# A hybrid attention and MoE block: when the softmax denominators are inverted, and how many at once

## The chip, the cores and the metric

The kernel runs on one core of one Trainium2 chip. The metric is device time in microseconds (us) of one execution, as the median of several runs. The core has a matrix engine (TensorE, PE), three elementwise engines (VectorE or DVE, ScalarE or ACT, GpSimd or POOL) and SyncE (SP), which issues DMA transfers. Each engine runs its own instructions in the order in which the program wrote them, and waits for others by semaphores.

## What is computed

One transformer block over 1024 tokens of width 1024. Two attention branches work on the same modulated input, are projected, gated, summed and projected once more; a mixture of experts follows. What matters here are the two softmaxes:

```python
# branch A: 4 heads, each with two maps m = 0, 1, over all visible keys
logits = jnp.where(visible, logits + bias[None, :, None], -jnp.inf)
p = jax.nn.softmax(logits, axis=-1)
attn = p[:, :, 0] - lam * p[:, :, 1]
return jnp.einsum('bhqs,bshe->bqhe', attn.astype(v.dtype), v)
# branch B: 8 heads, over the 256 keys that an indexer picked for the query
logits = jnp.where(sel_ok[:, None], logits - slopes[...] * dist[:, None], -jnp.inf)
p = jax.nn.softmax(logits, axis=-1)
return jnp.einsum('bhqk,bqkr->bqhr', p.astype(kv_sel.dtype), kv_sel)
# then
mixed = g[:, :, 0] * (y_a @ w_a_proj[l]) + g[:, :, 1] * (y_b @ w_b_proj[l])
x = _layer_norm(DEEPNORM_ALPHA * x + gate1 * (mixed @ w_o[l]), ln1_g[l], ln1_b[l])
```

A softmax needs the sum of each row's exponentials inverted. Branch A needs the inverse of two sums per row before it can subtract the maps. Branch B multiplies after the values: its output is scaled by the inverse sums.

## The kernel before

Everything is fp32. A product of two fp32 matrices is made as three matmuls (lines 142, 145, 146) of operands split into a high and a low part; `copy` makes the high part, mostly on ACT, and `sub` (line 128) the low part on DVE. A row block is 128 queries, so there are 8 of them, and a row of scores with a block's number `qb` has (qb + 1) x 128 columns.

**Branch A** (336 to 641 us of the span). `a_attend` (line 870) works head by head. For each of the 8 blocks `softmax_pair` makes the scores of both maps (PE `plg`), adds the bias and takes the row's extreme on DVE (line 762), and takes the exponential on ACT with the row's sum as a by-product (line 765). Then, per row block: a reciprocal of the first sum (line 879), a copy of the first map scaled by it on ACT (880), a reciprocal of the second sum (881), its product with minus lambda (`nlam`, 882), both of one column, and the subtraction of the maps over the whole row on DVE (883). PE turns the result by `ptr` (line 793), ACT and DVE split it (`pth`, `ptl`), and PE multiplies with the values (`py`). This work is woven (`weave`, with weights for each step) with the projections (`pj`) that branch B and the gates need; a scheduler sets the order of each engine's instructions from the order in which they are written and its own estimate of their durations.

At the end of the weave stand the last head of branch A, the last projections, and preparations of later stages, which the scheduler has pulled ahead: `gb`, a table of 128 x 8 modulation values, which is loaded from `mod_d` in DRAM (line 1355) and gets 1 added on DVE (line 1356); `wl`, the low half of projection weights; `hl`, the split of a projection for branch B's queries, written to DRAM as `bq` (lines 256, 257); `br` and `mod_d`, rows of the modulation (lines 710, 711).

**Branch B** (`b_stage`, line 939, 641 to 829 us). Eight heads in four pairs. Here the order is planned by hand: each step is a `node` with an engine, a duration, a priority and the nodes that it depends on, and takes and gives back buffers; the planner takes the node that can start earliest by these numbers, and of equals the one of the smallest priority. The instructions are then issued in just that order. Per row block: the scores (`plg`, lines 994 to 997), bias and extreme on DVE (1001), exponential on ACT with the sum (1014), a reciprocal of one column on DVE into `rden`, a table of 128 x 8 blocks x 8 heads (1017). Per two row blocks: `ptr` (1037), the split, and the values `pyb` (1054, 1055), then the output `yb` (1074). When a pair of heads is done, `scale(c)` (line 1084) spreads the inverse sums of half the rows over 128 x 512 elements (`rr`, line 1094), PE turns that (`pbc`, 1099), DVE multiplies the output with it (1103), and it is split into `ybh` and `ybl`. `of_pair` lists the nodes that `scale` depends on.

The planner also has **fill**, nodes of the lowest priority that PE is to do while it waits: the norm of branch A's output (`ya`, loaded from DRAM at line 1130, its PE step at 1146, its DVE step at 1150; `yah` and `yal` are its halves), and the first half of the output projection of branch A (`pab`, line 1198, 192 matmuls of 128 x 512), with `gate` at 1207.

**After branch B** comes the other half of that projection (`pab<-ybh`, lines 142 to 146), with weights `wab` that are loaded to a buffer of tag `wr` (two buffers), issued on ACT's queue (line 217). The two `rr` tiles use the same two buffers, so that load waits for the last `pbc`.

Of the kernel before, what the change touches and what calls it, by code (L numbers as in the profile page):

```python
# [19 lines left out]
AF = mybir.ActivationFunctionType  # L20
OP = mybir.AluOpType
# [65 lines left out]
def block_kernel(ctx: ExitStack, tc, a, out):  # L87
    nc = tc.nc
    V, S, G, PE = nc.vector, nc.scalar, nc.gpsimd, nc.tensor
# [8 lines left out]
    def s4(name, tag, shape=(128, 1024), dt=FT):  # L98
        return sb.tile(list(shape), dt, name=name, tag=tag, bufs=SLOTS[tag])
# [19 lines left out]
    def tiny(name, w=8, dt=FT, bufs=8, tag=None):  # L119
        return sb.tile([128, w], dt, name=name, tag=f"tiny{w}{tag or ''}", bufs=bufs)  # L120
# [618 lines left out]
    nlam = cp.tile([128, 1], FT, name="nlam")  # L739
# [9 lines left out]

    def softmax_pair(q, k, qs, bias, L):  # L750

        Ps, mx = [s4("P", "P") for _ in range(2)], [tiny("mx") for _ in range(2)]
        for n_, (c0, n) in enumerate(pieces(L)):
            ps_ = [bank("plg", "lg") for _ in range(2)]
            for m, (a_, b_) in enumerate(((1, 0), (0, 1), (0, 0))):
                for s, p in enumerate(ps_):
                    r = slice(64 * s, 64 * s + 64)
                    i = PE.matmul(p[:, :n], q[a_][r, qs], k[b_][r, c0:c0 + n], start=m == 0, stop=m == 2)  # L758
                    if m == 0:
                        leads(i)  # L760
            for P, mx_, p in zip(Ps, mx, ps_):
                V.tensor_tensor_reduce(P[:, c0:c0 + n], p[:, :n], bias[:, c0:c0 + n], 1.0, mx_[:, 5:6] if n_ else 3.0e38,  # L762
                                       OP.add, OP.min, mx_[:, 0:1] if n_ or L <= 512 else mx_[:, 5:6])
        for P, mx_ in zip(Ps, mx):
            S.activation(P[:, :L], P[:, :L], AF.Exp, bias=mx_[:, 0:1], scale=-1.0, accum_out=mx_[:, 1:2])  # L765
        return list(zip(Ps, mx))

    def softmax_rows(q, hh, ll, bias, L, sel=None):

# [100 lines left out]
    def a_attend(h):  # L870
        q, k, vh, vl = A.pop(h)
        bias = bias_tile(SL_A[h])

        def rows(qb):
            L = (qb + 1) * 128
            bv = bias[:, 896 - 128 * qb:1024]
            qs = slice(qb * 128, qb * 128 + 128)
            (P0, m0), (P1, m1) = softmax_pair(q, k, qs, bv, L)
            V.reciprocal(m0[:, 2:3], m0[:, 1:2])
            S.activation(P0[:, :L], P0[:, :L], AF.Copy, scale=m0[:, 2:3])  # L880
            V.reciprocal(m1[:, 2:3], m1[:, 1:2])
            V.tensor_tensor(m1[:, 3:4], m1[:, 2:3], nlam, op=OP.mult)
            V.scalar_tensor_tensor(P0[:, :L], P1[:, :L], m1[:, 3:4], P0[:, :L], op0=OP.mult, op1=OP.add)
            return P0

        def tail(i, Ps):
            y = bank("py", "av", (128, 256))
            last = 2 * i + 1
            for kb, c0, n, th, tl in transposed_pairs(Ps, i):
                if kb % 2 == 0 and kb:  # L890
                    yield True
                if kb == min(2, last):
                    mean_squares()
                kv_ = slice(kb * 128, kb * 128 + 128)
                mm3(y[:, c0:c0 + n], vh[:, kv_], vl[:, kv_], th, tl, kb == 0, kb == last)
            yo = sb.tile([128, 256], FT, name="yo", tag="yo", bufs=2)
            copy(yo, y)
            dma(ya_d[h, :, i * 256:i * 256 + 256], yo)
            sq = sb.tile([128, 256], FT, name="yq", tag="yo", bufs=2)
            V.tensor_scalar(sq, yo, 1.84e19, -1.84e19, op0=OP.min, op1=OP.max)  # L900
            S.activation(sq, sq, AF.Square)
            squares.append((h, i, sq))
            yield True

        return pipelined(rows, tail)


# [31 lines left out]
    def b_stage():  # L939
# [15 lines left out]
        def head(n):  # L955
            nonlocal prev_bias
            c, s = heads[n]
# [18 lines left out]
            def row(qb):  # L976
# [34 lines left out]

                def exp():
                    P, mx = st["P"], st["mx"]
                    S.activation(P[:, :L], P[:, :L], AF.Exp, bias=mx[:, 0:1], scale=-1.0, accum_out=mx[:, 1:2])  # L1014

                e = node("ACT", 0.42 + 0.00095 * L, prio, mins, exp)
                of_pair.append(node("DVE", 0.1, prio + 4, [e], lambda: V.reciprocal(rden[:, qb, n:n + 1], st["mx"][:, 1:2])))
                return st, e

            def tail(i, rows_):  # L1020
# [63 lines left out]
        def scale(c, prio, y):  # L1084
            for half in range(2):
# [3 lines left out]
                def spread(half=half, z=z):  # L1089
                    if half == 0:  # L1090
                        ybh[c], ybl[c] = s4("ybh", "L", dt=FR), s4("ybl", "L", dt=FR)
                    z["rr"] = s2("rr", "wr")
                    rr = rden[:, half * 4:half * 4 + 4, 2 * c:2 * c + 2].unsqueeze(3).to_broadcast([128, 4, 2, 64])
                    copy(z["rr"].rearrange("p (j s e) -> p j s e", j=4, s=2), rr, V)

                def turn(z=z):
# [1 line left out]
                    for j in range(4):  # L1098
                        PE.transpose(z["p"][:, j * 128:j * 128 + 128], z["rr"][:, j * 128:j * 128 + 128], ident)

                f = node("DVE", 0.45, prio, y, spread, take=("wr",))
                b = node("PE", 0.46, prio, [f], turn, take=("tp",), give=(("wr", f),))
                d = node("DVE", 0.69, prio, [b], lambda t=t, z=z: V.tensor_tensor(ybs[c][:, t], ybs[c][:, t], z["p"], op=OP.mult),
                         give=(("tp", b),))
# [967 lines left out]
```

## Time and profile before

| | us |
|---|---|
| median of 3 runs | 1365.82 |
| the 3 runs | 1362.2, 1365.85, 1365.82 |
| the profiled execution | 1362.08 |
| its span | 1360.3 |

| engine | busy us | share of the span |
|---|---|---|
| PE | 1228.1 | 90% |
| DVE | 950.2 | 70% |
| ACT | 665.4 | 49% |
| POOL | 128.1 | 9% |

The busy shares are averages over stages of different kinds. From 30 to 607 us PE is hardly ever idle. It idles around branch B's start and end, and again in the experts, from 850 us on. PE's clock was granted at full speed for 95.6% of the time. The profiled execution is one of the shorter ones, 3.7 us under the median.

### The profile page before, as it was taken

Reading aid. Unit: us, or ns where it says so; the run is one execution under the profiler, and the core shown is the slowest. Engines: PE = TensorE matmul, PEld = TensorE weight load, DVE = VectorE, ACT = ScalarE, POOL = GpSimd, SP = SyncE. Lnnn points to the kernel's source line nnn. Section 1 sums busy time; section 2 is a strip of 40 time slices with the busy share of each in tenths; the row PEclk is TensorE's granted clock in tenths of the full one; section 3 lists DMA queues with packets and bytes.
Section 4 is the critical chain, followed back from the end, with each engine's and each line's share of the span. In section 5 each row is a group of like instructions: output and inputs, shape, how many; then the busy total and the mean of one; then the engine's idle time right before and its main releaser. Section 6 shows DMA issues by size and latency. Waiting matters only on the chain.

```text
span 1360.3 us, 18426 instructions
## 1 busy us (share of the span) xinstructions
PE 1228.1 (90%) x6184; PEld 969.7 (71%) x6199; DVE 950.2 (70%) x2065; ACT 665.4 (49%) x1189; POOL 128.1 (9%) x154
## 2 busy tenths in 40 slices
PE   8999999999999999999699997898985898999940
PEld 6876678877777778677578886677873677788830
DVE  6537789783456757672698886677786778777736
ACT  4536662213785555453677762324224565555405
POOL 1000000000000001010011000000002233232210
PEclk9999999999999999999899998898996999999975
DMA  9202452123124326683455525564436789989756
GB/s 364 101 32 70 147 178 86 41 74 123 47 75 163 119 69 201 192 221 110 120 147 147 151 89 178 190 219 165 177 124 220 269 275 289 314 297 292 235 90 250
DMA packets 109526, 226.18 MB, mean 166 GB/s; under 512 B 34144, under 2 KB 40688, under 8 KB 109424
## 3 DMA queue, kind: packets, MB, share of 16 engines
q1 hardware_dynamic: 70144, 166.38, 34.8%
q0 software_dynamic: 35824, 52.23, 14.6%
q10 hardware_dynamic: 3456, 6.29, 1.5%
q8 instruction: 53, 0.87, 0.3%
q14 instruction: 49, 0.40, 0.1%
HBM read 170.15 MB, written 54.64 MB: 165 GB/s over the span
## 4 chain that ended last, share of the span: by engine, by line
PE 42%; DMA 20%; DVE 9%; issue 5%; ACT 2%; SPq 0%; POOLq 0%; another core or an unknown queue 0%; DVEq 0%; POOL 0%; ACTq 0%
DMA acc_d<-ot,idxs 7%; PE pj L142 4%; PE pj L146 4%; PE pj L145 4%; PE pab L1198 3%; PE plg L758 3%; DMA adaw<-ada_b 3%; PE ptr L1037 2%; PE po L142 2%; PE po L146 2%; PE po L145 2%; DMA raw<-w_o 2%; PE pgu L146 1%; PE pgu L142 1%; PE pgu L145 1%
## 5 line engine op out<-in xcount | busy, mean ns | idle before, releaser
L142 PE MATMUL pj<-uh,wl 128*128 128x512 f32 x544 | 219.5, 404 | 3.2 <-DVE hl L251 1.5
L145 PE MATMUL pj<-ul,wh 128*128 128x512 f32 x544 | 216.1, 397 | 0.0
L146 PE MATMUL pj<-uh,wh 128*128 128x512 f32 x544 | 216.1, 397 | 0.0
L128 DVE TENSOR_TENSOR ewl<-raw,ewh 128x1024 fp32r<-128x1024 f32 x102 | 122.7, 1220 | 32.3 <-ACT ewh L132 26.9
L132 ACT ACTIVATE ewh<-raw 128x1024 fp32r<-128x1024 f32 x102 | 105.6, 1057 | 57.5 <-DMA raw<-w_exp 53.5
L142 PEld LDWEIGHTS pj<-uh,wl 128*128 128x128 f32 x544 | 102.4, 188 | 35.3 <-issue 8.3
L146 PEld LDWEIGHTS pj<-uh,wh 128*128 128x128 f32 x544 | 102.5, 188 | 27.6 <-issue 7.2
L145 PEld LDWEIGHTS pj<-ul,wh 128*128 128x128 f32 x544 | 102.6, 189 | 24.5 <-issue 5.5
L132 ACT ACTIVATE pth<-ptr 128x512 fp32r<-128x512 f32 (+1 forms) x120 | 66.2, 553 | 63.6 <-PE ptr L1037 26.0
L128 DVE TENSOR_TENSOR ptl<-ptr,pth 128x512 fp32r<-128x512 f32 (+1 forms) x120 | 75.7, 633 | 22.6 <-ACT pth L132 22.2
L142 PE MATMUL pgu<-ewh,xl 128*128 128x512 f32 x200 | 81.2, 406 | 0.8 <-DVE xl L128 0.6
L146 PE MATMUL pgu<-ewh,xh 128*128 128x512 f32 x200 | 79.3, 397 | 0.0
L145 PE MATMUL pgu<-ewl,xh 128*128 128x512 f32 x200 | 79.2, 396 | 0.0
L765 ACT ACTIVATE P<-P,mx 128x128 f32<-128x128 f32 (+7 forms) x64 | 49.4, 773 | 44.4 <-DVE mx L762 41.4
L1840 POOL DMA_INDIRECT acc_d<-ot,idxs x24 | 47.0, 1960 | 186.3 <-DVE ot L1839 119.3
L128 DVE TENSOR_TENSOR wl<-raw,wh 128x512 fp32r<-128x512 f32 x68 | 44.8, 687 | 22.9 <-ACT wh L132 22.7
L758 PE MATMUL plg<-ak,aq 64*128 64x512 f32 (+4 forms) x288 | 57.2, 375 | 1.2 <-DVE mx L762 1.2
L142 PE MATMUL po<-woh,mxl 128*128 128x512 f32 x128 | 53.0, 415 | 5.6 <-DVE r L1422 4.2
L444 DVE SCALAR_TENSOR_TENSOR sc<-relu,iw,sc 128x512 f32<-128x512 f32 (+3 forms) x70 | 45.5, 654 | 17.8 <-ACT relu L439 15.8
L145 PE MATMUL po<-wol,mxh 128*128 128x512 f32 x128 | 51.3, 401 | 0.2 <-DVE wol L128 0.2
L146 PE MATMUL po<-woh,mxh 128*128 128x512 f32 x128 | 50.9, 401 | 0.0
L1014 ACT ACTIVATE P<-P,mx 128x128 f32<-128x128 f32 (+3 forms) x64 | 49.1, 769 | 2.9 <-DVE mx L1001 2.7
(440 smaller groups left out, 2896.3 us busy)
## 6 DMA issues: line engine op xcount, KB each, us to landing
raw<-w_exp SPq DMA_DIRECT2D x102, 512.0 KB
raw<-w_main SPq DMA_DIRECT2D x68, 256.0 KB
adaw<-ada_b SPq DMA_DIRECT2D x32, 512.0 KB
adaw<-ada_a SPq DMA_DIRECT2D x16, 512.0 KB
gates_d<-gt SPq DMA_DIRECT2D x32, 256.0 KB
gate<-gates_d SPq DMA_DIRECT2D x32, 256.0 KB
xt<-xT SPq DMA_DIRECT2D x8, 512.0 KB
bv_d<-bvs SPq DMA_DIRECT2D x16, 256.0 KB
```

Of the source, the lines that this page charges most:

```text
L128: e.tensor_tensor(o, i0, i1, op=OP.subtract)
L132: return S.activation(o, i, AF.Copy)
L142: i = PE.matmul(o, wl, xh, start=first, stop=False)
L145: PE.matmul(o, wh, xl, start=False, stop=False)
L146: e = PE.matmul(o, wh, xh, start=False, stop=last)
L444: V.scalar_tensor_tensor(acc, r[:, :n], w, acc, op0=OP.mult, op1=OP.add)
L758: i = PE.matmul(p[:, :n], q[a_][r, qs], k[b_][r, c0:c0 + n], start=m == 0, stop=m == 2)
L765: S.activation(P[:, :L], P[:, :L], AF.Exp, bias=mx_[:, 0:1], scale=-1.0, accum_out=mx_[:, 1:2])
L1014: S.activation(P[:, :L], P[:, :L], AF.Exp, bias=mx[:, 0:1], scale=-1.0, accum_out=mx[:, 1:2])
L1037: PE.transpose(p[:, k:k + 128], rows_[s_][0]["P"][:, kb * 128:kb * 128 + 128], ident)
L1198: PE.matmul(z["p"], w[:, cs], y[:, t], start=k + m == 0, stop=k == 3 and m == 2)
L1840: G.indirect_dma_start(out=acc_d, out_offset=bass.IndirectOffsetOnAxis(ap=isc, axis=0), in_=ot, in_offset=None, compute_op=OP.add)
```

## The change

Branch A: `softmax_pair` lets both exponentials write their sums into one small tile, side by side. One reciprocal of 128 x 2 inverts both. The copy of the first map on ACT is scaled by the first as before; the product of the second with minus lambda is a one-column copy on ACT with a scale, in place of a multiply on DVE; the subtraction of the maps follows on DVE. So a row has one reciprocal instead of two, one DVE multiply less and one ACT instruction more, and nothing of that is started before the second exponential is done.

Branch B: the exponential writes its sum straight into `rden`. The 64 reciprocals of one column are gone, with their nodes. `scale` inverts the sums of half the rows of a pair in one step, 128 x 4 x 2, in place, right before it spreads them: 8 reciprocals in all. Its node's duration goes from 0.45 to 0.6, and `of_pair` lists the exponentials where it listed the reciprocals.

```diff
--- before.py
+++ after.py
@@ -749,7 +749,8 @@
 
     def softmax_pair(q, k, qs, bias, L):
 
-        Ps, mx = [s4("P", "P") for _ in range(2)], [tiny("mx") for _ in range(2)]
+        Ps, sums = [s4("P", "P") for _ in range(2)], tiny("mx")
+        mx = [sums, tiny("mx")]
         for n_, (c0, n) in enumerate(pieces(L)):
             ps_ = [bank("plg", "lg") for _ in range(2)]
             for m, (a_, b_) in enumerate(((1, 0), (0, 1), (0, 0))):
@@ -761,9 +762,9 @@
             for P, mx_, p in zip(Ps, mx, ps_):
                 V.tensor_tensor_reduce(P[:, c0:c0 + n], p[:, :n], bias[:, c0:c0 + n], 1.0, mx_[:, 5:6] if n_ else 3.0e38,
                                        OP.add, OP.min, mx_[:, 0:1] if n_ or L <= 512 else mx_[:, 5:6])
-        for P, mx_ in zip(Ps, mx):
-            S.activation(P[:, :L], P[:, :L], AF.Exp, bias=mx_[:, 0:1], scale=-1.0, accum_out=mx_[:, 1:2])
-        return list(zip(Ps, mx))
+        for k, (P, mx_) in enumerate(zip(Ps, mx)):
+            S.activation(P[:, :L], P[:, :L], AF.Exp, bias=mx_[:, 0:1], scale=-1.0, accum_out=sums[:, 1 + k:2 + k])
+        return Ps, sums
 
     def softmax_rows(q, hh, ll, bias, L, sel=None):
 
@@ -875,12 +876,11 @@
             L = (qb + 1) * 128
             bv = bias[:, 896 - 128 * qb:1024]
             qs = slice(qb * 128, qb * 128 + 128)
-            (P0, m0), (P1, m1) = softmax_pair(q, k, qs, bv, L)
-            V.reciprocal(m0[:, 2:3], m0[:, 1:2])
-            S.activation(P0[:, :L], P0[:, :L], AF.Copy, scale=m0[:, 2:3])
-            V.reciprocal(m1[:, 2:3], m1[:, 1:2])
-            V.tensor_tensor(m1[:, 3:4], m1[:, 2:3], nlam, op=OP.mult)
-            V.scalar_tensor_tensor(P0[:, :L], P1[:, :L], m1[:, 3:4], P0[:, :L], op0=OP.mult, op1=OP.add)
+            (P0, P1), m = softmax_pair(q, k, qs, bv, L)
+            V.reciprocal(m[:, 3:5], m[:, 1:3])
+            S.activation(P0[:, :L], P0[:, :L], AF.Copy, scale=m[:, 3:4])
+            S.activation(m[:, 6:7], m[:, 4:5], AF.Copy, scale=nlam)
+            V.scalar_tensor_tensor(P0[:, :L], P1[:, :L], m[:, 6:7], P0[:, :L], op0=OP.mult, op1=OP.add)
             return P0
 
         def tail(i, Ps):
@@ -1011,10 +1011,10 @@
 
                 def exp():
                     P, mx = st["P"], st["mx"]
-                    S.activation(P[:, :L], P[:, :L], AF.Exp, bias=mx[:, 0:1], scale=-1.0, accum_out=mx[:, 1:2])
+                    S.activation(P[:, :L], P[:, :L], AF.Exp, bias=mx[:, 0:1], scale=-1.0, accum_out=rden[:, qb, n:n + 1])
 
                 e = node("ACT", 0.42 + 0.00095 * L, prio, mins, exp)
-                of_pair.append(node("DVE", 0.1, prio + 4, [e], lambda: V.reciprocal(rden[:, qb, n:n + 1], st["mx"][:, 1:2])))
+                of_pair.append(e)
                 return st, e
 
             def tail(i, rows_):
@@ -1090,7 +1090,9 @@
                     if half == 0:
                         ybh[c], ybl[c] = s4("ybh", "L", dt=FR), s4("ybl", "L", dt=FR)
                     z["rr"] = s2("rr", "wr")
-                    rr = rden[:, half * 4:half * 4 + 4, 2 * c:2 * c + 2].unsqueeze(3).to_broadcast([128, 4, 2, 64])
+                    both = rden[:, half * 4:half * 4 + 4, 2 * c:2 * c + 2]
+                    V.reciprocal(both, both)
+                    rr = both.unsqueeze(3).to_broadcast([128, 4, 2, 64])
                     copy(z["rr"].rearrange("p (j s e) -> p j s e", j=4, s=2), rr, V)
 
                 def turn(z=z):
@@ -1098,7 +1100,7 @@
                     for j in range(4):
                         PE.transpose(z["p"][:, j * 128:j * 128 + 128], z["rr"][:, j * 128:j * 128 + 128], ident)
 
-                f = node("DVE", 0.45, prio, y, spread, take=("wr",))
+                f = node("DVE", 0.6, prio, y, spread, take=("wr",))
                 b = node("PE", 0.46, prio, [f], turn, take=("tp",), give=(("wr", f),))
                 d = node("DVE", 0.69, prio, [b], lambda t=t, z=z: V.tensor_tensor(ybs[c][:, t], ybs[c][:, t], z["p"], op=OP.mult),
                          give=(("tp", b),))
```

Both orders are written by programs, so the change also moves instructions that it doesn't name. Three places follow; the new kernel's line numbers are one or two higher.

PE, the end of branch B, before: the last transposes of the inverse sums (`pbc<-ident,rr`), fill (`pab<-yah` and `pab<-yal`), and the first matmuls of the other half of the projection (`pab<-ybh`).

```order
L1198 MATMUL pab<-yah,wab 128x512 x2
L1099 MATMUL pbc<-ident,rr 128x128 x8
L1198 MATMUL pab<-yal,wab 128x512
L1198 MATMUL pab<-yah,wab 128x512 x2
L1198 MATMUL pab<-yal,wab 128x512
L1198 MATMUL pab<-yah,wab 128x512 x2
L1198 MATMUL pab<-yal,wab 128x512
L1198 MATMUL pab<-yah,wab 128x512 x2
L1198 MATMUL pab<-yal,wab 128x512
L1198 MATMUL pab<-yah,wab 128x512
L142 MATMUL pab<-ybh,wab 128x512
L145 MATMUL pab<-ybl,wab 128x512
```

The same place after, from the last value matmul (`pyb`) to the first matmuls of that other half:

```order
L1055 MATMUL pyb<-pth,bv 128x128
L1200 MATMUL pab<-yah,wab 128x512 x2
L1200 MATMUL pab<-yal,wab 128x512
L1200 MATMUL pab<-yah,wab 128x512 x2
L1200 MATMUL pab<-yal,wab 128x512
L1200 MATMUL pab<-yah,wab 128x512 x2
L1200 MATMUL pab<-yal,wab 128x512
L1200 MATMUL pab<-yah,wab 128x512
L1101 MATMUL pbc<-ident,rr 128x128 x8
L142 MATMUL pab<-ybh,wab 128x512
L145 MATMUL pab<-ybl,wab 128x512
L146 MATMUL pab<-ybh,wab 128x512
```

Before, eleven fill matmuls stand between the last `pbc` and the first `pab<-ybh`; after, none. In both orders ten stand between the last `pyb` and the last `pbc`. The eleven stand further ahead, among the matmuls of the last heads.

DVE, the end of the weave, before: from the last row of branch A (its reciprocals, `P<-P,mx 128x1024`) over `hl`, `wl` and the low halves of the turned rows (`ptl`) to branch B's start.

```order
L879 RECIPROCAL mx<-mx 128x1
L881 RECIPROCAL mx<-mx 128x1
L882 TENSOR_TENSOR mx<-mx,nlam 128x1
L710 TENSOR_TENSOR br<-pmr,br 1x512
L883 SCALAR_TENSOR_TENSOR P<-P,mx 128x1024
L251 SCALAR_TENSOR_TENSOR hl<-pj,hl 128x512
L128 TENSOR_TENSOR wl<-raw,wh 128x512 x2
L128 TENSOR_TENSOR ptl<-ptr,pth 128x384
L1356 TENSOR_SCALAR gb<-gb 128x8
L128 TENSOR_TENSOR ptl<-ptr,pth 128x512
L900 TENSOR_SCALAR yq<-yo 128x256
L128 TENSOR_TENSOR ptl<-ptr,pth 128x512
```

The same place after:

```order
L880 RECIPROCAL mx<-mx 128x2
L133 COPY yams<-prms 128x2
L251 SCALAR_TENSOR_TENSOR hl<-pj,hl 128x512
L128 TENSOR_TENSOR wl<-raw,wh 128x512 x2
L1358 TENSOR_SCALAR gb<-gb 128x8
L883 SCALAR_TENSOR_TENSOR P<-P,mx 128x1024
L128 TENSOR_TENSOR ptl<-ptr,pth 128x384
L900 TENSOR_SCALAR yq<-yo 128x256
L128 TENSOR_TENSOR ptl<-ptr,pth 128x512 x2
L133 COPY yams<-prms 128x2
L128 TENSOR_TENSOR ptl<-ptr,pth 128x512
L128 TENSOR_TENSOR ptl<-ptr,pth 128x384
```

The row's subtraction stood ahead of `hl`, `wl` and `gb`; now it stands behind all three, and `gb` directly ahead of it.

SP, the same place, before: the queue that issues the write of the modulation (`mod_d<-br`), of branch B's queries (`bq<-hl`), the load of `gb` and the loads of the fill's first weights (`raw<-w_ab`).

```order
L711 DMA mod_d<-br 1x512 x2
L256 DMA bq<-hl 128x512
L257 DMA bq<-hl 128x512
L1168 DMA raw<-w_ab 128x512
L1355 DMA gb<-mod_d 128x8x1
L1168 DMA raw<-w_ab 128x512
```

The same place after:

```order
L711 DMA mod_d<-br 1x512
L257 DMA bq<-hl 128x512
L711 DMA mod_d<-br 1x512
L256 DMA bq<-hl 128x512
L1357 DMA gb<-mod_d 128x8x1
L257 DMA bq<-hl 128x512
```

The load of `gb` stood behind the last write of `bq` and the first load of weights; now it stands ahead of both.

## Rows read from the trace of the kernel before

**Rows 1.** Windows: length, busy of PE, PEld, DVE, ACT, POOL, granted clock, DMA share, GB/s.

```profile
470.00:607.00 137.00, 135.77 (x694) 99.78 (x693) 96.58 (x245) 71.31 (x146) 7.27 (x12) 1.00 0.53 167
607.00:643.00 36.00, 33.20 (x167) 27.05 (x165) 8.20 (x19) 10.70 (x18) 1.62 (x2) 0.95 0.50 122
643.00:670.00 27.00, 18.35 (x108) 14.05 (x109) 17.97 (x57) 17.92 (x41) 2.35 (x3) 0.87 0.38 97
670.00:700.00 30.00, 24.86 (x172) 20.16 (x173) 26.44 (x76) 21.22 (x46) 3.10 (x6) 1.00 0.54 154
...
740.00:780.00 40.00, 39.86 (x261) 33.63 (x264) 33.80 (x98) 28.78 (x63) 4.22 (x7) 1.00 0.55 147
...
815.00:850.00 35.00, 27.62 (x133) 22.35 (x132) 22.05 (x36) 10.15 (x18) 0.00 (x0) 0.90 0.52 172
```

**Rows 2.** Groups by form: busy us, mean ns of one, idle time before them.

```profile
L1017 DVE RECIPROCAL rden<-mx 128x1 f32<-128x1 f32 x64 | 9.1, 154 | 1.0 <-ACT P L1014 0.9
...
L1120 ACT ACTIVATE yams<-yams 128x32 f32<-128x32 f32 x1 | 0.2, 229 | 0.0
```

**Rows 3.** Timeline of DVE at the start of branch B: start us, us, instruction.

```profile
645.48 0.16 DVE L1017 RECIPROCAL rden<-mx 128x1 f32<-128x1 f32 x1
645.56 0.47 DVE L1001 CUSTOM_DVE_ANT_0 P<-plg,bias 128x320 f32<-128x320 f32 x1
```

**Rows 4.** Timeline of DVE at the end of the weave.

```profile
604.90 0.16 DVE L881 RECIPROCAL mx<-mx 128x1 f32<-128x1 f32 x1 [0.97 <-ACT P L765]
605.10 0.16 DVE L882 TENSOR_TENSOR mx<-mx,nlam 128x1 f32<-128x1 f32 x1
...
606.89 1.28 DVE L883 SCALAR_TENSOR_TENSOR P<-P,mx 128x1024 f32<-128x1024 f32 x1 [0.46 <-ACT P L880]
615.30 0.69 DVE L251 SCALAR_TENSOR_TENSOR hl<-pj,hl 128x512 fp32r<-128x512 f32 x1 [7.12 <-DMA bq<-hl]
...
617.11 0.55 DVE L128 TENSOR_TENSOR ptl<-ptr,pth 128x384 fp32r<-128x384 f32 x1
625.11 0.17 DVE L1356 TENSOR_SCALAR gb<-gb 128x8 f32<-128x8 f32 x1 [7.46 <-DMA gb<-mod_d]
```

**Rows 5.** Timeline of PE at the same place.

```profile
612.38 0.49 PE L793 MATMUL ptr<-ident,P 128*128 128x128 f32 x3
...
616.04 0.50 PE L142 MATMUL pj<-uh,wl 128*128 128x512 f32 x1 [1.55 <-DVE hl L251]
...
619.04 0.28 PE L145 MATMUL py<-ptl,avh 128*128 128x256 f32 x1
...
625.93 0.39 PE L145 MATMUL py<-ptl,avh 128*128 128x256 f32 x1 [1.26 <-DVE ptl L128]
```

**Rows 6.** Timeline of SP's issues at the same place.

```profile
600.62 0.32 SPq L257 DMA_DIRECT2D bq<-hl  x1
...
617.05 0.39 SPq L1355 DMA_DIRECT2D gb<-mod_d  x1
```

**Rows 7.** Waits of DVE from 643 to 700 us: us in total, times, longest.

```profile
DVE ya L1150 <- DMA ya<-ya_d: 8.9, 4, 5.8
DVE rden L1017 <- ACT P L1014: 0.9, 1, 0.9
```

**Rows 8.** Timeline of PE from the last transposes of the denominators on.

```profile
828.85 1.04 PE L1099 MATMUL pbc<-ident,rr 128*128 128x128 f32 x8
...
830.42 0.39 PE L1198 MATMUL pab<-yal,wab 128*128 128x512 f32 x1
830.65 0.62 PE L1198 MATMUL pab<-yah,wab 128*128 128x512 f32 x2
...
836.32 0.80 PE L142 MATMUL pab<-ybh,wab 128*128 128x512 f32 x1 [3.92 <-DVE wab L128]
```

**Rows 9.** Timeline of DVE just ahead of them.

```profile
827.55 0.76 DVE L133 COPY rr<-rden 128x512 f32<-128x512 f32 x2
```

**Rows 10.** Timeline of ACT's queue at their end.

```profile
829.49 0.42 ACTq L217 DMA_DIRECT2D raw<-w_ab  x1
```
## Prediction

> **What bounds the kernel now.** I read the windows by stage first, because the share of busy time averages over stages with different limits. TensorE (PE) is the bound almost everywhere that the diff touches. In the stretch in which branch A runs woven with the projections, PE is busy 135.77 of 137 us; in branch B's middle 39.86 of 40 [rows 1]. There VectorE (DVE) is busy 70 to 85%, so taking instructions from it shortens nothing by itself. Three places around branch B are different, and there PE waits: the end of the weave (33.20 of 36 us), the start of branch B (18.35 of 27 and 24.86 of 30, so 8.65 + 5.14 = 13.8 us idle), and the end of branch B with the start of the output projection (27.62 of 35) [rows 1]. What the change is worth is decided in those three. So I read next the instructions of DVE, PE and the queues in time order there, and then what the diff does to the order of each engine.
>
> **Part 1, the instructions themselves.** Branch A has 32 rows (4 heads by 8 blocks). Each loses one of its two reciprocals (L881, 0.16 us) and the multiply L882 (0.16 us) [rows 4]; one reciprocal of two columns stays. ScalarE (ACT) gets 32 one-column copies; the trace has none of that form, the nearest is 0.229 us for 128x32 [rows 2], 7.3 us in all over 300 us in which ACT has time free (71 of 137 us busy [rows 1]). The first copy of a row must now wait for the second exponential. Both are covered by PE's queue of projection matmuls: PE lost 1.2 us in 137 us, so I take 0, with 1.5 us either way.
>
> Branch B loses 64 reciprocals L1017, 9.1 us of busy time at 154 ns each [rows 2]. What one costs in the queue is less: the reciprocal that starts at 645.48 is followed by the next instruction at 645.56, a step of 0.08 us [rows 3]. So 64 x 0.08 = 5.1 us of DVE's queue come free, some 24 of them (1.9 us) in the start of branch B, the only place where DVE, not PE, has a queue that others wait for. The Trainium skill, VectorE: DVE Perf Modes, "The DRAIN you can't avoid", says that the next instruction doesn't start until the pipeline of the one before is empty; by it each removed reciprocal would give its whole duration back, 24 x 0.154 = 3.7 us, and the forecast below would fall from 1368.0 to some 1366.2. The two rows just named speak against that for instructions that don't depend on each other.
>
> Eight reciprocals of 128x4x2 are added, each right in front of the copy that spreads it (L1094), which waits for it. Such a dependent step is 0.20 us: L881 starts at 604.90, L882, which reads it, at 605.10 [rows 4]. For the last pair both stand in front of the transposes that end branch B; the copies there are at 827.55 and their transposes start only at 828.85, behind ten fill matmuls [rows 8, 9]. Of the 0.4 us I take 0.2 on the path, with 0 and 0.4 as ends.
>
> **Part 2, the end of branch B.** The diff changes what the planner knows: 64 nodes of 0.1 us are gone, and the spreading nodes are 0.6 instead of 0.45. The plan comes out with the fill (the 192 matmuls of L1198) placed earlier. Before, 11 of them stand behind the last transposes of the denominators; after, none does, and the eleven stand ahead of branch B's last value matmul, in a stretch in which PE has no idle time to hide them. Each is a step of 0.23 us (830.42 to 830.65 [rows 8]), so 11 x 0.23 = 2.5 us later for the last transposes. That matters since the load of the next weights waits for them: it is issued on ACT's queue at 829.49 [rows 10], when the transposes give back the buffer, and everything behind it (the split on ACT and DVE, and PE's first matmul of the output projection at 836.32, after 3.92 us idle [rows 8]) hangs on that load. Before, the eleven fills ran in that idle time for nothing; after, it is empty. So +2.5 us, with PE idle 3.9 + 2.5 = about 6.5 us there. The ends: 0, if the fills find idle time in branch B after all, and +3.5 if the clock falls for longer behind the longer gap (0.90 of 35 us granted is 3.5 us lost now [rows 1]; I leave that loss as it is).
>
> **Part 3, the end of the weave.** Before, DVE stood still for 7.46 us on `gb`, a load issued at 617.05 that let it go at 625.11, some 8 us [rows 4, 6]; PE lost 1.26 us behind it, at 625.93 [rows 5]. In the new order `gb` stands in front of the last row of branch A (the scalar_tensor_tensor 128x1024, 1.28 us), where it stood behind it. That row was done at 608.2 (606.89 + 1.28 [rows 4]), long before its transposes at 612.38 [rows 5]. After, it can't start before 617.1 (`hl` at 615.30, then two `wl` [rows 4]) nor before `gb` lands. In its favour `gb` is issued earlier, behind the second write of `mod_d`, by my reckoning at 608 to 610; by the same 8 us it lands at 616 to 618, and the row is done at 618.5 to 619.5. PE comes to its transposes later than before: they now stand behind twelve projection matmuls and one of branch A that follow PE's own wait for `hl` (it ended at 616.04, and the thirteenth was through at 619.04 [rows 5]). So PE waits 0 to 0.8 us with the short split behind the row, and the 1.26 us of before go: I take -0.5. The low end is -3.1: no wait at all, and the clock loss of this stretch (0.95 granted over 36 us, 1.8 us [rows 1]) gone too. The high end goes by another load there: `bq` issued at 600.62 held `hl` until 615.30, 14.6 us [rows 4, 6]. By that `gb` lands at 622.6, the row is done at 624.0, and PE waits 5.0 us: +3.7 net.
>
> **Part 4, the start of branch B.** DVE waits here for the loads of `ya`, 8.9 us in four waits; it waited for an exponential ahead of L1017 only once, 0.9 us [rows 7]. The reciprocals' 1.9 us and that 0.9 go. But in the new order the fifth `ya` instruction stands further forward in DVE's queue than the load that it needs, whose buffer is freed by work just ahead of it: I reckon 2.9 us of new wait against the 2.8 gained. I take 0, with -1.5 and +1.5 as ends; the case beyond is the first rival. Behind branch B one split of the output weights moves ahead of a gate on DVE: less than 0.4 us, taken as 0.
>
> **Sum.** 0 + 0.2 + 2.5 - 0.5 + 0 = +2.2 us. Against the profiled execution (1362.08 us, of which the span is 1360.3) that is 1364.3. The profiled one lies 3.7 us under the median of 1365.82, as one of the three runs does (1362.2); the difference is the same for both kernels as far as I can tell, so the forecast for the median is 1365.8 + 2.2 = 1368.0. This kernel's runs can tell about 0.3% (4.1 us) from no change: the bounds for that are 1361.7 and 1369.9, and the forecast lies inside, nearer the upper one.
>
> **Rivals.**
> *The start of branch B gives back more (faster).* The loads of `ya` start 1 to 2 us sooner, since what frees their buffers moves up in DVE's shorter queue, and they land in time for the new order. Then the 8.9 us of waits and the 0.9 us go, and PE's 13.8 us idle fall by about as much; -9.8 + 2.2 = -7.6, 1358.2. For it: four of the eight loads wait for a buffer that DVE's own work frees. Against: the longest of the four waits, 5.8 us, is for the first loads [rows 7], which are issued before the removed instructions count for anything. It decides from 6.3 us gained on. Chance 0.20.
> *The late row holds PE (slower).* `gb` lands near 622, as `bq` did in the same congested stretch; +3.7 instead of -0.5 in part 3, and PE at half its clock for some us more behind that gap (I take 1.8 us, as much again as this stretch loses now [rows 1]): 0.2 + 2.5 + 3.7 + 1.8 = +8.2, 1374.0. For it: the load is of 4-byte pieces and is now issued while the 512 KB loads of branch B still run. Against: it took 8 us with DMA half busy [rows 1]. It decides from `gb` landing after about 620. Chance 0.18.
> *Nothing moves (no change).* The fills find idle time, or the load behind the transposes isn't what the output projection waits for: 0.2 - 0.5 = -0.3, 1365.5. Chance 0.12. That the exponentials now write straight into the table of denominators could also chain them to one another, each waiting for the last writer of that table; in the new order none waits for more than its own minimum, so I give this no chance of its own.
>
> **How the numbers follow.** Forecast 0.50, own range 1363.5 to 1372 (part 2 from 0.5 to 3.5, part 3 from -3.1 to +2). Faster by over 0.3%: nearly all of the first rival and a little of the forecast, 0.20. Slower by over 0.3%: the late row 0.18 and three tenths of the forecast, 0.33. Within 0.3%: the rest, 0.47. The range takes in most of both rivals, 1358 to 1375.
>
> **What would show it.** Right: the rows of L1017 gone with PE's busy share in the middle of branch B unchanged; no fill behind the last transposes of the denominators; the weights' load issued some 2 to 5 us later than 829.49 and PE idle about 6.5 us in front of the first output matmul; PE waiting at most 1 us on the last row's transposes near 619, with DVE's 7.5 us on `gb` cut to under 2. Wrong: the load at 829.5 or earlier (part 2 falls); PE idle under 8 us in the first 60 us of branch B (the first rival); a `gb` wait of over 5 us ahead of the last row (the second).

## The result, and the profile after

| | before | after |
|---|---|---|
| median us | 1365.84 | 1373.32 |
| ratio to before, 95% interval | | 1.0059 (1.003 to 1.0087) |
| profiled execution: us, span | 1362.08, 1360.3 | 1365.28, 1363.5 |

The change makes the kernel slower by 0.6%, some 8 us. The medians are of six runs each; one run of before took 2431 us, and the ratio leaves it out. The profiled execution of after is the shortest of its runs; a second trace of the same kernel, taken with the experiments, has a span of 1370.3 us, and a ratio of 1.0061 (1.0039 to 1.0082). I read both. The first is short by its experts: from the first to the last of their `pgu` matmuls it takes 254.9 us, the other thirteen traces 256.5 to 260.6, and the change touches nothing there.

The stages of after, first trace; columns as in [rows 1]:

```profile
470.00:607.00 137.00, 135.89 (x683) 99.61 (x684) 93.07 (x208) 71.24 (x159) 6.40 (x11) 1.00 0.52 162
607.00:643.00 36.00, 29.82 (x148) 24.63 (x147) 9.48 (x20) 12.31 (x21) 0.96 (x3) 0.91 0.49 121
643.00:670.00 27.00, 19.48 (x107) 14.37 (x105) 12.23 (x35) 14.30 (x28) 1.62 (x2) 0.87 0.37 102
670.00:700.00 30.00, 26.28 (x183) 21.01 (x183) 28.38 (x76) 24.95 (x57) 4.38 (x7) 1.00 0.63 163
740.00:780.00 40.00, 40.00 (x262) 33.64 (x261) 32.99 (x86) 28.52 (x61) 5.03 (x8) 1.00 0.55 150
815.00:850.00 35.00, 28.14 (x160) 23.60 (x159) 23.03 (x51) 14.29 (x28) 0.00 (x0) 0.90 0.42 141
```

Against [rows 1], the middle of branch B is as full as before (40.00 of 40 us). At the end of the weave PE is busy 29.82 of 36 us where it was 33.20, and its clock is granted 0.91 where it was 0.95. The two windows of branch B's start are a little fuller (19.48 and 26.28 us, against 18.35 and 24.86), though branch B starts some 7 us later in them.

What PE waits for from 600 to 720 us (us in total, times, longest) begins with an entry that the kernel before doesn't have:

```profile
PE ptr L794 <- DVE P L883: 6.2, 1, 6.2
PE pbc L1148 <- DVE ya L1152: 5.5, 1, 5.5
```

Here is how it comes about. DVE at the end of the weave, the rows that answer to [rows 4]:

```profile
612.75 1.29 DVE L128 TENSOR_TENSOR wl<-raw,wh 128x512 fp32r<-128x512 f32 x2
625.46 0.17 DVE L1358 TENSOR_SCALAR gb<-gb 128x8 f32<-128x8 f32 x1 [11.43 <-DMA gb<-mod_d]
625.54 1.28 DVE L883 SCALAR_TENSOR_TENSOR P<-P,mx 128x1024 f32<-128x1024 f32 x1
626.74 0.55 DVE L128 TENSOR_TENSOR ptl<-ptr,pth 128x384 fp32r<-128x384 f32 x1
```

SP's issues at the same place, which answer to [rows 6]:

```profile
608.70 0.24 SPq L711 DMA_DIRECT2D mod_d<-br  x1
612.13 0.32 SPq L256 DMA_DIRECT2D bq<-hl  x1
615.82 0.37 SPq L1357 DMA_DIRECT2D gb<-mod_d  x1
```

What SP's queue itself waited for from 595 to 632 us, of which one entry concerns `gb` (us in total, times, longest):

```profile
SPq L1357 <- DMA mod_d<-br: 3.3, 1, 3.3
```

PE, which answers to [rows 5], and ACT's last preparation of the row:

```profile
626.88 0.69 PE L794 MATMUL ptr<-ident,P 128*128 128x128 f32 x2 [6.18 <-DVE P L883]
```

```profile
614.09 0.28 ACT L882 ACTIVATE mx<-mx,nlam 128x1 f32<-128x1 f32 x1
```

DVE is through with `wl` at 614.0 and then stands for 11.43 us on `gb`. The last row of branch A, whose factor ACT had ready at 614.37, starts at 625.54 behind it, and PE's transposes of that row at 626.88, after 6.18 us without work. The load was issued at 615.82, 7.1 us behind the second write of `mod_d` at 608.70, which stores what it reads. A write of `bq` in front of it on SP's queue went out at 612.13, and then SP stood for 3.3 us until the write of `mod_d` had landed, by the entry above; so that landing, and not `bq`, set when the load could go. The other three traces with `gb` ahead of the last row have the same entry, with 1.9, 4.1 and 2.5 us (after_again, plan_kept, a_only). From its issue to DVE's release the load took 9.6 us.

The clock falls in such a gap and stays low behind it. Windows of the second trace, columns as in [rows 1] (the granted clock is the third number from the end):

```profile
618.00:622.00 4.00, 4.00 (x19) 3.11 (x17) 0.00 (x0) 0.60 (x1) 0.00 (x0) 1.00 0.97 243
622.00:626.00 4.00, 0.13 (x1) 0.00 (x0) 0.00 (x0) 0.00 (x0) 0.00 (x0) 0.93 0.79 166
626.00:630.00 4.00, 0.24 (x1) 0.24 (x2) 1.66 (x3) 0.00 (x0) 0.00 (x0) 0.50 0.41 142
630.00:634.00 4.00, 4.00 (x16) 3.53 (x16) 1.85 (x4) 1.68 (x4) 0.00 (x0) 0.50 0.11 39
634.00:636.00 2.00, 2.00 (x6) 1.55 (x6) 0.00 (x0) 0.00 (x0) 0.00 (x0) 0.58 0.00 0
636.00:640.00 4.00, 4.00 (x23) 3.39 (x21) 0.00 (x0) 0.60 (x1) 0.00 (x0) 1.00 0.17 66
```

PE has next to no work from 622 to 629.7. Its clock is granted 0.50, the lower of its two levels (1.2 GHz), from 626 on, and stays there to 634 and a little beyond, while PE works: some 3 us of work lost, (1 - 0.50) x 4 us + (1 - 0.58) x 2 us. These figures are means of the granted clock. So is the 0.956 of the kernel before (its `PEclk` over the whole span): with a lower level of 0.50 it means full speed for some 91% of the time, and not for 95.6%, as I wrote above.

The end of branch B, which answers to [rows 8, 9, 10], on PE, DVE and ACT's queue:

```profile
836.41 1.04 PE L1101 MATMUL pbc<-ident,rr 128*128 128x128 f32 x8
844.30 0.79 PE L142 MATMUL pab<-ybh,wab 128*128 128x512 f32 x1 [6.86 <-DVE wab L128]
```

```profile
835.09 0.20 DVE L1094 RECIPROCAL rden<-rden 128x8 f32<-128x8 f32 x1
835.33 0.43 DVE L133 COPY rr<-rden 128x512 f32<-128x512 f32 x1
835.67 0.19 DVE L1094 RECIPROCAL rden<-rden 128x8 f32<-128x8 f32 x1
835.90 0.43 DVE L133 COPY rr<-rden 128x512 f32<-128x512 f32 x1
```

```profile
837.04 0.39 ACTq L217 DMA_DIRECT2D raw<-w_ab  x1
```

The new reciprocals take 0.20 us each and their copies start 0.24 us behind them. The load of the weights goes out at 837.04, as the transposes end, and PE waits 6.86 us in front of the first output matmul, where it waited 3.92.

The added instructions of branch A and the new reciprocals, as groups (columns as in [rows 2]):

```profile
L882 ACT ACTIVATE mx<-mx,nlam 128x1 f32<-128x1 f32 x32 | 9.0, 280 | 0.0
```

```profile
L880 DVE RECIPROCAL mx<-mx 128x2 f32<-128x2 f32 x32 | 5.3, 164 | 18.8 <-ACT P L766 18.5
...
L1094 DVE RECIPROCAL rden<-rden 128x8 f32<-128x8 f32 x8 | 1.6, 199 | 0.0
```

### The profile page after: what moved, and what is told of

The parts are those of the page before. It is cut to its first block, busy times and chain, and to the rows that moved or that the text cites. A ratio compares the mean times of both kernels' runs of the same rounds, so it can differ in the third digit from the quotient of the medians.

```text
span 1363.5 us, 18355 instructions
## 1 busy us (share of the span) xinstructions
PE 1231.4 (90%) x6199; PEld 973.5 (71%) x6199; DVE 940.2 (69%) x1945; ACT 670.1 (49%) x1221; POOL 127.6 (9%) x154
## 3 DMA queue, kind: packets, MB, share of 16 engines
q0 software_dynamic: 35824, 52.23, 14.6%
## 5 line engine op out<-in xcount | busy, mean ns | idle before, releaser
L142 PEld LDWEIGHTS pj<-uh,wl 128*128 128x128 f32 x544 | 102.6, 189 | 34.0 <-issue 10.3
```

The costliest lines, as they stand in the source:

```text
L142: i = PE.matmul(o, wl, xh, start=first, stop=False)
```

## The stages of all runs

From the timelines of PE I took five moments of each traced kernel: the first and the last projection matmul (`pj`), the first fill matmul (`pab<-yah`), the end of the last transposes of the denominators (`pbc<-ident,rr`), and the last matmul of the output projection (`po`). The table gives the differences in us, and the ratio of the whole time to the kernel before, with its interval. "gb ahead" means that DVE's instruction on `gb` stands ahead of branch A's last row.

| kernel | gb | plan of B | weave | to first fill | to last `pbc` | to last `po` | ratio |
|---|---|---|---|---|---|---|---|
| before | behind | old | 590.2 | 59.2 | 129.6 | 181.6 | 1 |
| after | ahead | new | 594.4 | 57.1 | 132.1 | 181.4 | 1.0059 |
| after_again | ahead | new | 597.6 | 58.5 | 132.1 | 178.8 | 1.0061 (1.0039 to 1.0082) |
| plan_kept | ahead | old | 597.4 | 62.0 | 129.6 | 180.1 | 1.0057 (1.0034 to 1.0079) |
| a_only | ahead | old | 596.1 | 62.9 | 129.6 | 178.7 | 1.0072 (1.0042 to 1.0101) |
| b_only | behind | new | 588.3 | 56.1 | 132.1 | 179.7 | 0.9973 (0.995 to 0.9996) |
| gb_late | away | new | 590.6 | 58.5 | 132.1 | 179.9 | 0.9991 (0.9968 to 1.0014) |
| gb_late_again | away | new | 587.7 | 59.6 | 132.1 | 179.0 | 0.9977 (0.9955 to 0.9999) |
| gb_late_plan_kept | away | old | 587.8 | 65.3 | 129.6 | 180.9 | 0.9996 (0.9976 to 1.0016) |
| before_gb_late | away | old | 585.4 | 60.2 | 129.6 | 179.3 | 0.9979 (0.9957 to 1.0) |
| a_part_gb_late | away | old | 587.3 | 63.2 | 129.6 | 179.8 | 0.9978 (0.9956 to 0.9999) |
| b_part_gb_late | away | new | 584.6 | 57.9 | 132.1 | 180.8 | 0.9956 (0.993 to 0.9982) |
| fill_held | away | new, held | 586.3 | 59.5 | 130.8 | 180.9 | 0.9956 (0.993 to 0.9982) |
| b_part_gb_late_held | away | new, held | 588.9 | 57.4 | 130.8 | 179.4 | 0.994 (0.9917 to 0.9964) |

Each trace is one execution: the same kernel's stage moves by 1 to 3 us (after and after_again, gb_late and gb_late_again). Only the stretch from the first fill to the last `pbc`, in which PE is hardly ever idle, repeats to 0.05 us.

## Experiments

**The changed kernel again, as a base.** 

> The changed kernel once more, as the base for the three runs beside it on the same chip. In its first trace PE waited 6.2 us for the last row of branch A (gb landed at 625.5), PE's wait ahead of the first output matmul was 6.9 us instead of 3.9, and the first projection matmul started 2.9 us later than before. Theory (the gb load ahead of the last row costs about 5 us, the fill moved ahead of the last transposes 2.5): the ratio to the kernel before is about 1.006 again, PE's wait for the last row between 4 and 8 us. Rival (the two traces differ mostly by how the first loads happened to run): the first projection matmul starts at 51 like before, and the ratio is nearer to 1.003.

PE waited 7.6 us for the last row; the weave took 597.6 us. The ratio of 1.006 repeats. The first projection matmul started at 54.3 as in the first trace, but that tells nothing of the change: in the fourteen traces it starts at 51.0 to 51.8 or at 53.6 to 55.2, and a_only, which has the changed order, is among the early ones, while before_gb_late, whose PE order is that of before, is among the late ones.

**gb out of the way.** 

> The changed kernel with the addition of 1 to gb folded into the two later instructions that use it, so that DVE has no instruction on gb ahead of the last row of branch A. PE's order is that of the changed kernel, row for row. Theory: PE's wait of 6.2 us for the last row falls below 1.5 us, and the time by 4 to 6 us against the changed kernel, to a ratio of about 1.002 to 1.003 to the kernel before. Rival (the row is late for other reasons, or branch B's start, which waits for loads, takes the gain back): the wait goes, the time falls by less than 2 us.

```diff
-    V.tensor_scalar(gb[:, 0], gb[:, 0], 1.0, None, op0=OP.add)
     tc8 = tiny("tc8")
-    V.tensor_tensor(tc8, smalls[:, 34:42], gb[:, 0], op=OP.mult)
+    V.scalar_tensor_tensor(tc8, gb[:, 0], 1.0, smalls[:, 34:42], op0=OP.add, op1=OP.mult)
     V.tensor_tensor(gb[:, 1], gb[:, 1], tc8, op=OP.add)
-    V.tensor_tensor(gb[:, 0], gb[:, 0], smalls[:, 26:34], op=OP.mult)
+    V.scalar_tensor_tensor(gb[:, 0], gb[:, 0], 1.0, smalls[:, 26:34], op0=OP.add, op1=OP.mult)
```

The two remaining instructions stand in branch B, hundreds of rows later. The time fell by 9 us on the same chip (1372.07 to 1362.95 in the medians), more than the 4 to 6 expected, and all that the change had cost. DVE and PE at the same place:

```profile
616.13 1.28 DVE L883 SCALAR_TENSOR_TENSOR P<-P,mx 128x1024 f32<-128x1024 f32 x1 [0.38 <-ACT mx L882]
617.34 0.55 DVE L128 TENSOR_TENSOR ptl<-ptr,pth 128x384 fp32r<-128x384 f32 x1
```

```profile
622.41 0.38 PE L794 MATMUL ptr<-ident,P 128*128 128x128 f32 x2
```

The last row starts at 616.13, as soon as ACT has made its factor, and PE comes to its transposes at 622.41 without a wait. The window from 607 to 643 us is full, and at full clock:

```profile
607.00:643.00 36.00, 36.00 (x190) 29.38 (x190) 11.72 (x27) 14.35 (x25) 4.45 (x7) 1.00 0.56 137
```

**Branch B's old plan.** 

> The changed kernel, but branch B's planner is told of the 64 nodes of 0.1 us and of 0.45 for the spreading step as before; the nodes issue nothing. So branch B's order is that of the kernel before, less the reciprocals: 171 fill matmuls ahead of the last value matmul, 11 behind the last transposes. Theory: PE's wait ahead of the first output matmul goes back from 6.9 to about 4 us, the time falls by 2 to 3 us against the changed kernel (ratio about 1.004), and the start of branch B loses or gains under 1.5 us. Rival (the new plan's gain at the start of branch B, about 2 us between the two traces, is given back): the time is that of the changed kernel within 1 us.

```diff
-                of_pair.append(e)
+                of_pair.append(node("DVE", 0.1, prio + 4, [e], lambda: None))
...
-                f = node("DVE", 0.6, prio, y, spread, take=("wr",))
+                f = node("DVE", 0.45, prio, y, spread, take=("wr",))
```

The eleven fill matmuls went back behind the last transposes, and the stretch to the last `pbc` from 132.1 to 129.6 us: the 2.5 us are there to the tenth. Yet the time is the same (1372.07 both). The rival is right: the start of branch B loses what the end gains, 62.0 us to the first fill instead of 58.5. The reason shows on DVE. In the new plan (after_again), the first `ya` instruction, the first low half `yal` that gives back a `ya` buffer, and the fifth `ya`, which needs it:

```profile
660.47 0.75 DVE L1152 SCALAR_TENSOR_TENSOR ya<-ya,smalls,pbc 128x512 f32<-128x512 f32 x1 [1.10 <-PE pbc L1148]
...
674.78 0.69 DVE L128 TENSOR_TENSOR yal<-ya,yah 128x512 fp32r<-128x512 f32 x1
...
679.76 0.74 DVE L1152 SCALAR_TENSOR_TENSOR ya<-ya,smalls,pbc 128x512 f32<-128x512 f32 x1
```

The same three in the old plan (plan_kept):

```profile
660.16 0.75 DVE L1152 SCALAR_TENSOR_TENSOR ya<-ya,smalls,pbc 128x512 f32<-128x512 f32 x1 [1.05 <-PE pbc L1148]
...
676.75 0.68 DVE L128 TENSOR_TENSOR yal<-ya,yah 128x512 fp32r<-128x512 f32 x1
...
685.24 0.75 DVE L1152 SCALAR_TENSOR_TENSOR ya<-ya,smalls,pbc 128x512 f32<-128x512 f32 x1 [1.22 <-DMA ya<-ya_d]
```

From the first `ya` on, `yal` comes after 14.3 us instead of 16.6, the load behind it starts earlier, and the fifth `ya` comes after 19.3 us without a wait instead of 25.1 us with one.

**Both.** 

> Both edits in one. Theory (the two terms add): 7 to 8 us under the changed kernel, a ratio of 0.999 to 1.001 to the kernel before, since the fewer instructions on DVE are worth 0 to 2 us. Rival (only one of the two counts): no faster than the better of the two alone.

0.9996, no faster than gb_late alone: the two don't add. The plan's two effects are there again, 65.3 us to the first fill instead of 58.5 and 59.6, and 129.6 instead of 132.1 us to the last `pbc`.

**Branch A's part alone.** 

> Branch A's part of the change alone; branch B with its 64 reciprocals and its planner as before. The order at the end of the weave is that of the changed kernel, with gb ahead of the last row. Theory (the gb load holding the last row is the whole loss): PE waits 6 to 8 us for the last row, a ratio of 1.005 to 1.007 to the kernel before, as the changed kernel. Rival (branch B's part has a share): under 1.004.

1.0072. PE waited 6.8 us for the last row, DVE 11.6 us on `gb`. Branch A's part alone carries the whole loss.

**Branch B's part alone.** 

> Branch B's part of the change alone; branch A as before, so gb stands behind the last row. Theory: no wait of PE for the last row; from the first fill matmul to the end of the last transposes of the denominators 132.1 us instead of 129.6 (the eleven fill matmuls), of which the start of branch B and the later weight loads give most back: a ratio of 0.999 to 1.002. Rival (the 2.5 us are lost in full): 1.002 or more, with the time from the last transposes to the end unchanged. Other rival (the reciprocals' removal speeds branch B's start by 3 us or more): under 0.998.

0.9973, a gain of 3.7 us that is just clear of none. The stretch to the last `pbc` is 132.1 us, but the start of branch B takes 56.1 us, the shortest of all. The ratio is the one that the other rival named; its reason, the reciprocals themselves, isn't shown by this run, which has the new plan too.

**The kernel before with gb out of the way.** 

> The kernel before, with the addition of 1 to gb folded into the two later instructions, as in gb_late. PE's order is that of the kernel before, row for row. Theory: DVE's 7.5 us on gb go, and with them PE's wait of 1.3 us at 626 and the fall of the clock behind it (0.66 of 5 us, 1.7 us): 1 to 3 us less, a ratio of 0.998 to 0.999. Rival (branch B's start waits for ya loads whatever the weave does): the weave ends earlier, branch B's start gives it back, 1.000.

0.9979 (0.9957 to 1.0): in the expected place, at the edge of what can be told. The weave took 585.4 us where the trace of before has 590.2. So `gb` seems to have cost the kernel before something already, some 3 us by the ratio: PE's 1.26 us of [rows 5] are gone, and the clock from 607 to 643 us is granted 1.00 instead of 0.95. The lower clock doesn't always follow: b_only has the same wait of 1.3 us, at a clock of 1.00. With `gb` out of the way on both sides the change makes no difference that can be told: gb_late has 0.9991 and 0.9977, this kernel 0.9979.

**The fill held back.** 

> gb_late, with the last 21 fill matmuls held back by dependencies: 171 ahead of the last value matmul, 10 between it and the last transposes, 11 behind these, as before; the rest of the new plan of branch B is kept. Theory (the load behind the last transposes counts, but the next weights' wait gives more than half of it back, as the two plans' waits of 12.5 and 14.8 us show): the last transposes 2.5 us earlier, PE's waits for weights behind them 1 to 2 us shorter in all, the time 0.5 to 1.5 us under gb_late. Rival (all behind it hangs on that load, as the prediction has it): 2.5 us or more under gb_late. Other rival (the next stage's loads set the end): no difference.

```diff
+                        late_ = c * 24 + half * 12 + k * 3 + m
+                        after_ = turned[-1] if late_ >= 181 else valued[-1] if late_ >= 171 else None
-                        x = node("PE", 0.23, FILL, [x, wl_, normed[2 * k + half], before_f], mm, ...
+                        x = node("PE", 0.23, FILL, [x, wl_, normed[2 * k + half], before_f, after_], mm, ...
```

Here `turned` lists the nodes of the denominators' transposes and `valued` the last value matmuls of each two row blocks. The last transposes came only 1.3 us earlier (130.8 us), not 2.5: PE waited 0.4 us in two places of that stretch where fill had stood, and the rest I haven't traced. The ratio is 0.9956, that of gb_late 0.9991 and 0.9977: the intervals overlap, so a gain is possible and not shown.

**gb_late again.** 

> gb_late (both parts of the change, gb not ahead of the last row) once more, as the base for the three runs beside it on the same chip: a ratio of 0.996 to 1.000 to the kernel before.

0.9977, in the expected place.

**Branch A's part without gb in the way.** 

> Branch A's part alone, with gb not ahead of the last row. Theory (all that branch A's part costs is the place of gb; its fewer instructions are covered by PE): the weave takes 585 to 591 us as in the kernels without that wait, and the time is that of the kernel before with gb late, a ratio of 0.996 to 1.000. Rival (the later first copy of each row, which now waits for both exponentials, costs of its own): the weave is 2 us or more longer than 591, a ratio over 1.001.

0.9978, the same as before_gb_late, which differs from it by nothing but branch A's part. So once `gb` is away that part gains and costs nothing that these runs can tell (their intervals are 3 us to either side). The weaves agree: 587.9 us in the mean of the five traces with branch A's part and `gb` away, 586.3 in the three without it, closer than two traces of one kernel. So neither the fewer instructions on DVE nor the later first copy of each row counts here; that PE's queue covers both is the likely reason.

**Branch B's part without gb in the way.** 

> Branch B's part alone, with gb not in DVE's way. Theory (branch B's part gains 3 to 4 us, gb out of the way 2 to 3, and the two add): a ratio of 0.994 to 0.996. From the end of the weave to the first fill matmul 56 to 59 us, as in the other kernels with the new plan, against 59 to 65 with the old one. Rival (both gain the same wait for the ya loads): 0.997 to 0.998.

0.9956: the two gains add, as far as the intervals tell.

**The same with the fill held back.** 

> b_part_gb_late with the last 21 fill matmuls held back as in fill_held. Theory (the fill's 2.5 us come back in part): 0 to 1.5 us under b_part_gb_late, a ratio of 0.993 to 0.996. Rival (the next weights' wait gives all of it back): no difference from b_part_gb_late.

0.994 (0.9917 to 0.9964), the best of all, 0.6% under the kernel before. That the held fill has a share in it isn't shown: the interval of b_part_gb_late overlaps.

## Why the prediction came out as it did

The measured median lies 5.3 us over the forecast. It is outside the forecast's own range (1363.5 to 1372) and inside the whole one (1358 to 1375), which reached that far only for the second rival's sake. The side that had a chance of 0.33, slower by over 0.3%, came true, and the likeliest, no change that can be told, did not. By its steps:

**Part 1, the instructions.** Right in sum. The weave takes 584.6 to 590.6 us with branch A's part or without it, if `gb` is out of the way or behind the last row. The one-column copy on ACT is dearer than the row that I took: 0.280 us instead of 0.229, 9.0 us in all, and still covered. The removed reciprocals of branch B are worth nothing that shows on their own: a_only and plan_kept have the same plan of branch B, one with and one without them, and take 62.9 and 62.0 us to the first fill, less apart than two traces of one kernel; a_part_gb_late and gb_late_plan_kept are another such pair, and there the one with the reciprocals is the shorter (63.2 and 65.3). My step of 0.08 us was one row taken for all 64. In the trace of before 33 of the reciprocals stand singly, with a follower that isn't marked as waiting: 21 are followed after 0.07 to 0.08 us, 12 after 0.18 to 0.25, 0.13 in the mean, so the 5.1 us should have been some 8. The runs don't tell either from the whole duration, which the Trainium skill, VectorE: DVE Perf Modes, "The DRAIN you can't avoid", would give back for an instruction that is held; that an instruction which isn't held starts earlier is said in the same section, so my two rows didn't speak against it. The dependent step took 0.24 us instead of 0.20.

**Part 2, the fill.** Right in place and size: 132.1 - 129.6 = 2.5 us, in every pair of kernels that differ in the plan. What follows the last `pbc` takes as long with either plan (178.7 to 181.6 us with the old one, 178.8 to 181.4 with the new one; in the mean 180.1 and 179.9), so the delay goes through to the end of the output projection, as I had said. A time of its own the runs don't give it: plan_kept gives the 2.5 us back in the start of branch B, and fill_held moved the last transposes by only 1.3. PE's wait in front of the first output matmul was forecast as 6.5 us and was 6.9. The load of the weights went out 7.6 us later than before (837.04), not 2 to 5: the weave had ended 7.1 us later too.

**Part 3, the end of the weave: here the prediction failed.** I took -0.5 us, and in the second rival +3.7 or, with the clock, +5.5. The weave takes 594.4 to 597.6 us in the four traces with `gb` ahead, 596.4 in the mean, and 589.3 in the two with `gb` behind (before and b_only): +7.1 us. The second rival's mechanism, place and sign were right, and what decided was the step on when `gb` lands. I had it issued at 608 to 610, 1.5 to 3.5 us behind the second write of `mod_d` (606.46 in the trace of before); it was 5.7 to 7.9 us behind that write in the four traces, since the load waits until the write has landed, and I had not asked how long that takes. From issue to release I took the 8 us of before; it was 9.5 to 12.1 us. So `gb` let DVE go at 624.3 to 628.3 where I had 616 to 618, and PE waited 6.2, 7.6, 7.4 and 6.8 us where I had allowed 0 to 0.8, and 5.0 in the worst case. The clock cost some 3 us in after_again against (1 - 0.95) x 36 = 1.8 us before [rows 1], less than the 1.8 more that I had put on it.

**Part 4, the start of branch B.** The sum was about right, its making wrong. With the whole change the start takes 57.1 to 59.6 us where it took 59.2 and 60.2 (before and before_gb_late), -1.1 us in the mean of five and two traces, within my -1.5 to +1.5. But the fifth `ya` that I made wait for 2.9 us doesn't wait: the work that gives back its buffer has moved forward too, as the first rival had it. With branch A as before the new plan gains some 2 to 3.5 us here (56.1, 57.9 and 57.4). With branch A's part and the old plan the start takes longer, 62.0 to 65.3 us in four traces. A part of that is longer waits of DVE for the loads of the second and the fifth `ya`: 7.3 to 10.3 us together in these four, 6.7 and 6.6 in before and before_gb_late. Why the loads come later behind branch A's new order isn't shown.

**The sum.** +7.1 at the weave, -1.1 at branch B's start, +2.5 from the fill: +8.5 against a measured 0.0059 x 1365.8 = 8.1 us. The forecast of +2.2 had -0.5 for the first of these. The second rival's 1374.0 is within 0.7 us of the measured median partly by luck: its +5.5 for the weave was 1.6 too small, and it left out the 1.1 us that branch B's start gave back.

**The chances.** The late row had 0.18. By the rows at hand it deserved more: a transfer of its stretch, `bq`, had taken 14.6 us by my own reading [rows 4, 6], and I took the 8 us of a later stretch as the likely value for a load that moved into this one.

## What to carry to other kernels

When a change moves an instruction that waits for a load ahead of one on which another engine depends, its price is set by when the load can be issued and how long it takes there. So follow the issuing queue row by row, ask what the load itself must wait for (here the landing of a write to DRAM), and take the nearest duration from the same stretch. A small operation on a loaded table can be folded into its later users, which takes the wait out of the engine's queue; here that was worth 9 us behind the change, and some 3 us, at the edge of what can be told, without it. And an order that a planner makes from durations moves far-off work when nodes are taken away: the fill moved for a loss of 2.5 us and the buffers came back earlier for a gain of about as much, while the removed instructions themselves counted for nothing that the runs tell.

## What the runs showed of the hardware

The load of `gb`, 4 KB in pieces of four bytes, took 8.1 us from its issue to DVE's release in both traces in which it stands behind the last row, and 9.5, 9.6, 10.7 and 12.1 us in the four in which it stands ahead. The mean busy share of DMA over these times is 0.68 in the two, and 0.74, 0.75, 0.77 and 0.78 in the four, in the same order. That the busier DMA makes the load longer is argued from these six alone. The load waited in SP's queue for the landing of a write of 2 KB, which came 5.7 to 7.9 us behind that write's issue.

In the traces with `gb` ahead PE's clock was at its lower level while PE still waited, and for 4 to 6 us of work behind the wait, in a stretch that gb_late runs at 1.00 throughout.
